# Two query tiles of a pair of heads at once in the attention of a two-layer hybrid block

## The chip, the cores and the metric

The kernel runs on one core of one Trainium2 chip. The metric is the device time of one execution in microseconds; the median of three runs of the kernel before is 2845.89 us (2841.22 to 2847.46).

## What is computed

Two layers over 256 latent tokens x and 256 context tokens ctx, width 1024, all in fp32. The part that matters here is the attention of the mixer, cut from the reference:

```python
for l in range(DEPTH):
    ...                                   # adaLN tables, first feed-forward part
    q, k, v, z, xbc, dt, g = split_in(h @ w_in[l])     # for latents and for context
    # 16 heads of 64; q and k normalised, latents rotated
    # latents: each query sees a window of latent keys (with a bias and a mask) and all context keys
    s_all = concat([q . k_win * scale + bias (or -inf), q . k_ctx * scale])
    o_l = softmax(s_all) . [v_win, v_ctx]
    # context, in layer 0 only: queries see the context keys
    o_c = softmax(q_c . k_c * scale) . v_c
    ...                                   # state-space branch, gates, output, second feed-forward part
```

## The kernel before, in words

Matrix products are made of three products of fp32r halves: `wchunk` (L85 to L92) splits each chunk of weights into a high and a low part, by a copy on ScalarE (L90) and a subtraction on VectorE (L91), and `gemm_t` and `gemm_n` (L114 to L116, L125 to L127) issue three matmuls per step.

PSUM has eight banks. Three form the ring "mm" (`bank`, L130), one the ring "ms" (`bank2`, L133). In attention a score tile "s" has two banks and one buffer, and "o" has two buffers of one bank (`pbank`). A ring hands out a bank for each tile that is asked for and takes it back when the last reader of the tile before is done. The ring "mm" serves qkps (the q, k and v products), qkt (their transposes), gps (gates), dtps (the step sizes of the state-space branch) and nps (the output product with na_w_o). Within block 0 some qkps and qkt tiles take "o" banks instead (L447).

The 16 heads are worked in four blocks of four (L633 to L637). `qkv_block` makes q, k and v of a block from 256 columns of w_in each, normalises and rotates q and k, and transposes them; at its end (L521 to L524) it makes the first q product of the next block ahead. In block 0, `gates(0, 2)` follows; then `attend`. After the four blocks come `dt_prep` and `gates(2, 4)` (L639, L640) and the product with na_w_o (L647).

`attend` takes a pair of heads c, a segment s (0: latent queries against 512 keys; 1: context queries against 256, in layer 0 only) and a query tile qt of 128 at a time. `scores` makes the two score products of the pair (L574; each head has 64 rows of the array), adds the bias and mask for segment 0 (L576), and calls `softmax`: one maximum over both heads (L551), and per head an exponential with its sum (L555), a reciprocal (L556) and a scaling (L557). `outputs` transposes the probabilities in blocks of 128 (L592, into an "ms" bank), copies them to SBUF (L593), and after the second query tile makes the products with v of both heads (L599, into an "o" bank) and splits the result into halves (L330, L331). The loop at L607 calls `scores` one step ahead of `outputs`.

The order of the instructions on each engine is fixed when the program is built. The instructions that are ready go in the order of the program text, so that products traced later stand between pieces of attention that still wait. On TensorE's list the score products of a step wait until the exponentials of the step before have read the score tile.

Of the kernel before, what the change touches and what calls it, by code (L numbers as in the profile page):

```python
# [7 lines left out]
F32 = mybir.dt.float32  # L8
# [3 lines left out]
ALU = mybir.AluOpType  # L12
# [4 lines left out]
P = 128  # L17
# [3 lines left out]
T = 512  # L21
SEG = 256
DFF = 2816
KF = DFF // P
HD = 64
# [31 lines left out]
class Kernel:  # L57
    def __init__(self, tc, I, dbg):
        self.tc, self.nc, self.I, self.dbg = tc, tc.nc, I, dbg
        self.ada_it, self.ada_done, self.wnext = self.ada_all(), (-1, 0), None  # L60

    def dump(self, name, ap):
        if self.dbg is not None and name in self.dbg:
            self.nc.sync.dma_start(self.dbg[name], ap)
# [373 lines left out]
    def qkv_block(self, l, b, ap, tabs, ctx_q, ahead):  # L438


        nc = self.nc
# [4 lines left out]
        qk = ap.tile([P, 4, T], F32, name="qk", tag="qk", bufs=2)  # L446
        v = ap.tile([P, 4, 256], F32, name="v", tag="v", bufs=2)  # L447

        tags = iter("mmmooommmoo" if b == 0 else "m" * 11)

        def bank(n):
            return self.bank(n) if next(tags) == "m" else self.pbank("o", 2)

        def products(t2, w):
            ps = bank("qkps").rearrange("p (a n) -> p a n", a=2)
            for i in range(2):
                self.gemm_n(ps[:, i], w, 0, 256, self.hrhs, slice((2 * t2 + i) * P, (2 * t2 + i + 1) * P))
            return ps

        def finish(t2, a, ps):  # L460

            p3 = ps.rearrange("p t (h d) -> p (t h) d", d=HD)
            sq = ap.tile([P, 2, 256], F32, name="sq", tag="sq").rearrange("p t (h d) -> p (t h) d", d=HD)
            nc.scalar.activation(sq, p3, AF.Square)
            ss = self.sm.tile([P, 8], F32, name="ss", tag="ss")
            nc.vector.tensor_reduce(out=ss, in_=sq, axis=AX.X, op=ALU.add)
            r = self.rstd(ss, 8, HD)
            qn = ap.tile([P, 2, 256], F32, name="qn", tag="qn")
            q3 = qn.rearrange("p t (h d) -> p (t h) d", d=HD)
# [12 lines left out]
            pt = bank("qkt").rearrange("p (c t n) -> p c t n", c=2, t=2)  # L482
            for t in range(2):
                for c in range(2):
                    nc.tensor.transpose(pt[:, c, t], qn[:, t, c * P : (c + 1) * P], self.con("id"))
            o = qk[:, 2 * a : 2 * a + 2, t2 * SEG : (t2 + 1) * SEG].rearrange("p c (t n) -> p c t n", t=2)
            nc.scalar.copy(o, pt[:, :, :, ::-1] if t2 == 0 and a == 0 else pt)
# [55 lines left out]
                                in1=self.con("mask")[:, None, :].to_broadcast([P, 12, GRID]), op=ALU.add)  # L543
        return bt

    def softmax(self, ap, ps, nk):

        nc = self.nc
        mx = self.sm.tile([P, 2], F32, name="mx", tag="mx", bufs=4)
        sm = self.sm.tile([P, 2], F32, name="sme", tag="sme", bufs=4)  # L550
        nc.vector.tensor_reduce(out=mx, in_=ps, axis=AX.X, op=ALU.max, negate=True)  # L551
        out = []
        for a in range(2):
            p = ap.tile([P, T], F32, name="p", tag="p", bufs=3)[:, :nk]
            self.last_exp = nc.scalar.activation(p, ps[:, a], AF.Exp, bias=mx[:, a : a + 1], accum_out=sm[:, a : a + 1]).ins  # L555
            nc.vector.reciprocal(sm[:, a : a + 1], sm[:, a : a + 1])  # L556
            nc.vector.tensor_scalar(out=p, in0=p, scalar1=sm[:, a : a + 1], scalar2=None, op0=ALU.mult)  # L557
            out.append(p)
        return out

    def attend(self, l, b, ap, qk, v, ctx_q, aT):
        nc = self.nc
        units = [(c, s, a, qt) for c in range(2) for s in range(2 if ctx_q else 1) for qt in range(2) for a in range(2)]
        bts, st, pts = {}, {}, {}

        def scores(us):
            c, s, _, qt = us[0]
# [3 lines left out]
            ps = self.pph.tile([P, 2, T], F32, name="ps_s", tag="s", bufs=1)[:, :, : nk * P]  # L571
            for a in range(2):
                o = slice(64 * a, 64 * a + 64)
                nc.tensor.matmul(ps[:, a], qk[o, c, (2 * s + qt) * P : (2 * s + qt + 1) * P], qk[o, 2 + c, s * SEG :], start=True, stop=True)  # L574
            if s == 0:
                nc.vector.tensor_tensor(out=ps[:, :, :SEG], in0=ps[:, :, :SEG],  # L576
                                        in1=bts[c][:, :, 2 - 2 * qt : 6 - 2 * qt].rearrange("p a e k -> p a (e k)"), op=ALU.add)
            for u, p in zip(us, self.softmax(ap, ps, nk * P)):
                st[u] = p

        def outputs(us):

            c, s, _, qt = us[0]
            nk = 4 if s == 0 else 2
            if qt == 0:
                for a in range(2):
                    pts[a] = ap.tile([P, 4, SEG], F32, name="pt", tag="pt", bufs=2)[:, :nk]
            for u in us:
                p = st.pop(u)
                tp = self.bank2("ptp").rearrange("p (j q) -> p j q", j=4)[:, :nk]  # L590
                for j in range(nk):
                    nc.tensor.transpose(tp[:, j], p[:, j * P : (j + 1) * P], self.con("id"))  # L592
                last = nc.scalar.copy(pts[u[2]][:, :, qt * P : (qt + 1) * P], tp[:, :, ::-1] if s == 0 else tp).ins  # L593
            if qt == 1:
                po = self.pbank("o", 2)[:, :SEG]
                for j in range(nk):
                    for a in range(2):
                        hc = (2 * c + a) * HD
                        i = nc.tensor.matmul(po[64 * a : 64 * a + 64], v[:, j + 4 - nk, hc : hc + HD], pts[a][:, j], start=(j == 0),  # L599
                                             stop=(j == nk - 1), tile_position=(0, 64 * a)).ins  # L600
                        if j == a == 0:
                            self.tc.add_manual_dep(i, last.name, mybir.DependencyInfo(
                                mybir.DependencyClass.Sync, mybir.DependencyReason.DATA), reason="pairs")
                self.split(aT[2 * b + c][:, :, s * SEG : (s + 1) * SEG], po)
# [575 lines left out]
```

## Time and profile before

| what | value |
|---|---|
| runs | 2841.22, 2845.89, 2847.46 us; median 2845.89 |
| profiled execution | 2845.74 us, its span 2844.0 us, mean granted clock 0.991 |
| TensorE busy | 2752.6 us, 97% of the span |
| VectorE busy | 2007.0 us, 71% |
| ScalarE busy | 1344.2 us, 47% |
| chain that ended last | TensorE 85%, VectorE 6%, DMA 4%, ScalarE 3% |
| score products (L574) | 96 products, 192 records |
| transposes of p (L592) | 320 records |
| products with v (L599) | 320 records |

An fp32 product appears as two records of the array (two passes), a transpose or an fp32r product as one. A busy TensorE is not TensorE at its peak, as the ends of pipelined matmuls are modelled; distances between starts tell more than durations. "qkps" and the like are the program's names for tiles.

### The profile page before, as it was taken

The page shows a single profiled execution, that of the slowest core. Times are in us where ns is not written, and L with a number is a line of the kernel's source. Part 1 is how long each engine was busy: PE and PEld are TensorE (multiplying, and loading weights), DVE is VectorE, ACT ScalarE, POOL GpSimd, SP SyncE. Part 2 cuts the span into 40 slices and gives each one's busy share as a digit, 9 for nine tenths or more (in the row PEclk, how much of TensorE's full clock was granted, in tenths as well). Part 3 has the DMA queues.
Part 4 walks back from the last instruction along what each step waited for, and adds up shares of the span by engine and source line. Part 5 has one row for each costly group of instructions (what it writes and reads, how often), then busy time and mean ns, then how long its engine had stood idle before and what let it go on. Part 6 is the DMA issues. An engine that isn't in the chain of part 4 may idle for free.

```text
span 2844.0 us, 41229 instructions
## 1 busy us (share of the span) xinstructions
PE 2752.6 (97%) x15748; PEld 2274.6 (80%) x15748; DVE 2007.0 (71%) x3793; ACT 1344.2 (47%) x2453; POOL 76.9 (3%) x132
## 2 busy tenths in 40 slices
PE   7999999999999999998999999999899999999899
PEld 5888888776777777787888898888888787789899
DVE  5995356767479888779963389533687868898654
ACT  4322233544368887643312242222344558777443
POOL 0000010100000000000000000000100000000000
PEclk9999999999999999999999999999999999999999
DMA  8874253321322222365743267432544343335564
GB/s 284 263 242 126 85 157 97 77 55 43 118 73 58 72 63 89 104 207 186 236 155 89 93 197 242 130 94 89 163 114 91 65 144 92 90 117 164 163 186 148
DMA packets 316246, 374.21 MB, mean 132 GB/s; under 512 B 15504, under 2 KB 292368, under 8 KB 315664
## 3 DMA queue, kind: packets, MB, share of 16 engines
q1 hardware_dynamic: 308624, 351.64, 40.5%
q0 software_dynamic: 7424, 19.93, 3.8%
q8 instruction: 124, 2.03, 0.3%
q14 instruction: 74, 0.61, 0.1%
HBM read 363.13 MB, written 8.39 MB: 131 GB/s over the span
## 4 chain that ended last, share of the span: by engine, by line
PE 85%; DVE 6%; DMA 4%; ACT 3%; issue 1%; POOL 0%; SPq 0%; ACTq 0%; DVEq 0%; POOLq 0%
PE pg L115 5%; PE pg L114 5%; PE pg L116 5%; PE pd L116 5%; PE pd L115 5%; PE pd L114 5%; PE pu L115 5%; PE pu L116 5%; PE pu L114 5%; PE xps L114 3%; PE xps L115 3%; PE xps L116 3%; PE ps_y L846 3%; PE qkps L125 2%; PE qkps L127 2%; PE qkps L126 2%
## 5 line engine op out<-in xcount | busy, mean ns | idle before, releaser
L91 DVE TENSOR_TENSOR hl<-raw,hl 128x1024 fp32r<-128x1024 f32 (+1 forms) x538 | 624.1, 1162 | 468.0 <-ACT hl L90 466.5
L90 ACT CAST hl<-raw 128x1024 fp32r<-128x1024 f32 (+1 forms) x538 | 537.1, 1001 | 659.5 <-PE pd L116 246.7
L192 DVE SCALAR_TENSOR_TENSOR junk<-wt,cb 128x1024 f32<-128x1024 f32 x256 | 312.5, 1221 | 7.8 <-DMA wt<-in_w_adt_dram 3.4
L116 PE MATMUL pd<-act,hl 128*128 128x512 f32 (+1 forms) x824 | 277.3, 336 | 0.0
L115 PE MATMUL pd<-act,hl 128*128 128x512 f32 (+1 forms) x824 | 276.6, 336 | 0.0
L114 PE MATMUL pd<-act,hl 128*128 128x512 f32 (+1 forms) x824 | 276.1, 335 | 0.0
L114 PE MATMUL pg<-h,hl 128*128 128x512 f32 (+1 forms) x736 | 264.5, 361 | 8.5 <-ACT h L330 4.8
L116 PE MATMUL pg<-h,hl 128*128 128x512 f32 (+1 forms) x736 | 265.0, 360 | 1.0 <-DVE hl L91 1.0
L115 PE MATMUL pg<-h,hl 128*128 128x512 f32 (+1 forms) x736 | 265.4, 361 | 0.5 <-DVE h L331 0.5
L114 PE MATMUL pu<-h,hl 128*128 128x512 f32 (+1 forms) x696 | 252.9, 364 | 0.7 <-DVE x L325 0.7
L115 PE MATMUL pu<-h,hl 128*128 128x512 f32 (+1 forms) x696 | 253.1, 364 | 0.0
L116 PE MATMUL pu<-h,hl 128*128 128x512 f32 (+1 forms) x696 | 252.8, 363 | 0.0
L126 PE MATMUL qkps<-hl,h 128*128 128x256 f32 x672 | 194.2, 289 | 7.7 <-DVE hl L91 7.7
L125 PE MATMUL qkps<-hl,h 128*128 128x256 f32 x672 | 195.8, 292 | 4.9 <-ACT hl L90 3.8
L127 PE MATMUL qkps<-hl,h 128*128 128x256 f32 x672 | 193.1, 287 | 0.0
L873 DVE SCALAR_TENSOR_TENSOR m<-m,dtn,cbm 128x256 f32<-128x256 f32 (+1 forms) x384 | 144.6, 411 | 36.1 <-ACT m L871 35.6
L115 PEld LDWEIGHTS pd<-act,hl 128*128 128x128 f32 x824 | 154.8, 188 | 18.1
L114 PEld LDWEIGHTS pd<-act,hl 128*128 128x128 f32 x824 | 154.9, 188 | 17.9
L116 PEld LDWEIGHTS pd<-act,hl 128*128 128x128 f32 x824 | 155.0, 188 | 16.5
L114 PEld LDWEIGHTS pg<-h,hl 128*128 128x128 f32 x736 | 138.8, 190 | 33.0 <-ACT h L330 6.5
L115 PEld LDWEIGHTS pg<-h,hl 128*128 128x128 f32 x736 | 139.7, 190 | 24.2 <-DVE h L331 2.2
L116 PEld LDWEIGHTS pg<-h,hl 128*128 128x128 f32 x736 | 139.6, 190 | 24.3 <-DVE hl L91 1.2
(270 smaller groups left out, 5981.9 us busy)
## 6 DMA issues: line engine op xcount, KB each, us to landing
raw<-in_w_in_dram SPq DMA_DIRECT2D x144, 512.0 KB, 3.9
wt<-in_w_adt_dram SPq DMA_DIRECT2D x128, 512.0 KB, 4.4
raw<-in_ffn_w_down_dram SPq DMA_DIRECT2D x92, 512.0 KB, 3.5
raw<-in_ffn_w_gate_dram SPq DMA_DIRECT2D x88, 512.0 KB, 3.9
raw<-in_ffn_w_up_dram SPq DMA_DIRECT2D x88, 512.0 KB, 3.9
raw<-in_ssd_w_o_dram SPq DMA_DIRECT2D x32, 512.0 KB, 3.5
raw<-in_w_out_dram SPq DMA_DIRECT2D x20, 512.0 KB, 4.0
wa<-in_w_ada_dram SPq DMA_DIRECT2D x16, 512.0 KB, 8.9
```

The source lines that it names most:

```text
L90: nc.scalar.copy(hl[:, 0], t)
L91: nc.vector.tensor_tensor(out=hl[:, 1], in0=t, in1=hl[:, 0].bitcast(F32), op=ALU.subtract)
L114: mm(ps, wh, xh[:, cols], start=(first and i == 0), stop=False)
L115: mm(ps, wh, xl[:, cols], start=False, stop=False)
L116: mm(ps, wl, xh[:, cols], start=False, stop=(last and i == len(st) - 1))
L125: mm(ps, xh[:, cols], wh, start=(i == 0), stop=False)
L126: mm(ps, xh[:, cols], wl, start=False, stop=False)
L127: mm(ps, xl[:, cols], wh, start=False, stop=(i == len(st) - 1))
L192: nc.vector.scalar_tensor_tensor(out=self.junk, in0=w, scalar=1.0, in1=self.cb[:, s], op0=ALU.mult, op1=ALU.mult, accum_out=md[:, k, s : s ...
L846: nc.tensor.matmul(*a, **k)
L873: v.scalar_tensor_tensor(out=e[:, o1], in0=e[:, o1], scalar=self.dtn[:, 2 * s + j, r : r + 1], in1=cbm[s][:, d, o1], op0=ALU.mult, op1=ALU ...
```

## The change

`attend` works on a pair of heads and a segment, with both query tiles at once. `scores` issues four score products in a row. For segment 0 they go to two score tiles of two banks each; for segment 1 all four share one tile (each bank holds the two query tiles of a head). The first of the four waits for the last exponential of the unit before, and stands behind the last product with v issued so far. `softmax` takes two heads, or for segment 1 all four rows at once with one maximum. The score tag "s" has two buffers, and "o" is gone: the products with v take a bank of "mm", and so do the transposes of the second head of each query tile. In block 0, qkps and qkt tiles that took "o" banks take halves of "s" tiles. Probability tiles have four buffers for three.

```diff
@@ qkv_block
+        spare = []
+
         def bank(n):
-            return self.bank(n) if next(tags) == "m" else self.pbank("o", 2)
+            if next(tags) == "m":
+                return self.bank(n)
+            if not spare:
+                two = self.pph.tile([P, 2, T], F32, name="ps_o", tag="s", bufs=2)
+                spare.extend([two[:, 1], two[:, 0]])
+            return spare.pop()
@@ softmax
-    def softmax(self, ap, ps, nk):
+    def softmax(self, ap, ps, n):
...
-        for a in range(2):
-            p = ap.tile([P, T], F32, name="p", tag="p", bufs=3)[:, :nk]
+        for a in range(n):
+            p = ap.tile([P, T], F32, name="p", tag="p", bufs=4)[:, :nk]
@@ attend
-        units = [(c, s, a, qt) for c in range(2) for s in range(2 if ctx_q else 1) for qt in range(2) for a in range(2)]
+        units = [(c, s) for c in range(2) for s in range(2 if ctx_q else 1)]
...
+            if s == 0:
+                ps = [self.pph.tile([P, 2, T], F32, name="ps_s", tag="s", bufs=2) for _ in range(2)]
+            else:
+                p4 = self.pph.tile([P, 2, T], F32, name="ps_s", tag="s", bufs=2).rearrange("p a (q n) -> p a q n", q=2)
+                ps = [p4[:, :, qt] for qt in range(2)]
+            for qt in range(2):
+                for a in range(2):
+                    o = slice(64 * a, 64 * a + 64)
+                    i = nc.tensor.matmul(ps[qt][:, a], qk[o, c, ...], qk[o, 2 + c, s * SEG :], start=True, stop=True).ins
+                    if st and qt == a == 0:
+                        self.tc.add_manual_dep(i, self.last_exp.name, ... Sync ...)
+                        if self.last_pv:
+                            self.tc.add_manual_dep(i, self.last_pv.name, ... NoSync ...)
+            for qt in range(2):
+                if s == 0:
+                    nc.vector.tensor_tensor(out=ps[qt][:, :, :SEG], ... bias ...)
+                    for a, p in enumerate(self.softmax(ap, ps[qt], 2)):
+                        st[c, s, qt, a] = p
+            if s == 1:
+                for i, p in enumerate(self.softmax(ap, p4.rearrange("p a q n -> p (a q) n"), 4)):
+                    st[c, s, i % 2, i // 2] = p
...
-                tp = self.bank2("ptp").rearrange("p (j q) -> p j q", j=4)[:, :nk]
+                    tp = (self.bank("ptp") if a else self.bank2("ptp")).rearrange("p (j q) -> p j q", j=4)[:, :nk]
...
-                po = self.pbank("o", 2)[:, :SEG]
+            po = self.bank("ps_o")[:, :SEG]
...
+                    self.last_pv = i
...
-        for i in range(0, len(units) + 2, 2):
+        for i in range(len(units) + 1):
             if i < len(units):
-                scores(units[i : i + 2])
+                scores(units[i])
             if i > 0:
-                outputs(units[i - 2 : i])
+                outputs(units[i - 1])
```

## Rows read from the trace of the kernel before

**Rows 1.** The page: busy time by engine; the chain that ended last by engine.

```profile
PE 2752.6 (97%) x15748; PEld 2274.6 (80%) x15748; DVE 2007.0 (71%) x3793; ACT 1344.2 (47%) x2453; POOL 76.9 (3%) x132
...
PE 85%; DVE 6%; DMA 4%; ACT 3%; issue 1%; POOL 0%; SPq 0%; ACTq 0%; DVEq 0%; POOLq 0%
```

**Rows 2.** Windows of both attention stretches: length, busy time by engine with records.

```profile
core 0: us, PE busy (x) PEld busy (x) DVE busy (x) ACT busy (x) POOL busy (x), PEclk, DMA share, GB/s
492.00:727.10 235.10, 224.86 (x1519) 170.59 (x1518) 167.15 (x411) 119.85 (x278) 15.53 (x24) 1.00 0.29 61
2102.60:2273.70 171.10, 164.30 (x1217) 134.41 (x1216) 132.25 (x290) 87.31 (x169) 15.81 (x24) 1.00 0.40 83
sum 406.20, PE 389.16 PEld 305.00 DVE 299.40 ACT 207.16 POOL 31.34; mean PE 194.58 PEld 152.50 DVE 149.70 ACT 103.58 POOL 15.67
```

**Rows 3.** Timeline of TensorE in block 0 of layer 0: start, duration, line.

```profile
523.18 1.13 PE L574 MATMUL ps_s<-qk 64*128 64x512 f32 x4
524.24 0.66 PE L592 MATMUL ptp<-c_cst,p 128*128 128x128 f32 x4
524.65 0.36 PE L127 MATMUL qkps<-hl,h 128*128 128x256 f32 x1
...
525.63 0.66 PE L592 MATMUL ptp<-c_cst,p 128*128 128x128 f32 x4
...
528.36 0.70 PE L574 MATMUL ps_s<-qk 64*128 64x256 f32 x4
...
531.73 0.70 PE L574 MATMUL ps_s<-qk 64*128 64x256 f32 x2
532.36 1.95 PE L599 MATMUL ps_o<-pt,v 128*64 128x256 f32 x16
534.23 0.70 PE L574 MATMUL ps_s<-qk 64*128 64x256 f32 x2
534.86 0.44 PE L592 MATMUL ptp<-c_cst,p 128*128 128x128 f32 x2
```

**Rows 4.** Windows of TensorE where products stand alone (256, then 512 columns).

```profile
659.90:669.20 9.30, 9.30 (x80) 1.00 0.33 89
727.00:768.00 41.00, 41.00 (x180) 1.00 0.39 122
```

**Rows 5.** Timeline of TensorE at the start of block 3's attention, layer 0.

```profile
669.17 0.60 PE L485 MATMUL qkt<-c_cst,qn 128*128 128x128 f32 x4
671.37 0.63 PE L485 MATMUL qkt<-c_cst,qn 128*128 128x128 f32 x4 [1.60 <-DVE qn L481]
671.75 0.47 PE L114 MATMUL dtps<-h,hl 128*64 128x512 f32 x1
```

**Rows 6.** Timeline of VectorE: the second chunk of dtps's weights is split.

```profile
625.63 0.42 DVE L91 TENSOR_TENSOR hl<-raw,hl 128x256 fp32r<-128x256 f32 x1
```

**Rows 7.** Timeline of ScalarE: the copy of v out of its bank.

```profile
669.37 0.59 ACT L490 COPY v<-qkps 128x512 f32<-128x512 f32 x1 [4.17 <-PE qkps L127]
```

**Rows 8.** Groups by line and form, 492 to 727: count, busy us, mean ns, idle before.

```profile
L551 DVE TENSOR_REDUCE mx<-ps_s 128x2 f32<-128x1024 f32 x16 | 19.5, 1220 | 0.3
...
L593 ACT COPY pt<-ptp 128x512 f32<-128x512 f32 x32 | 18.8, 588 | 25.6 <-PE ptp L592 25.6
...
L557 DVE TENSOR_SCALAR p<-p,sme 128x512 f32<-128x512 f32 x32 | 15.3, 482 | 0.9
...
L555 ACT ACTIVATE p<-ps_s,mx 128x256 f32<-128x256 f32 x32 | 15.0, 475 | 2.7 <-DVE mx L551 1.9 <-PE ptp L592 0.7
...
L576 DVE TENSOR_TENSOR ps_s<-ps_s,bt 128x512 f32<-128x512 f32 x16 | 11.1, 694 | 7.0 <-PE ps_s L574 7.0
```

**Rows 9.** Line L555, the exponentials: ns least, median, most.

```profile
L555 ACT ACTIVATE p<-ps_s,mx x96: 465/682/704, 499.2 to 2261.2; 128x512 f32<-128x512 f32 x64, 128x256 f32<-128x256 f32 x32
L555 ACT ACTIVATION_READ_ACCUMULATOR p<-ps_s,mx x96: 190/200/220, 499.7 to 2261.8; 128x1 f32 x96
...
L555 ACT ACT_TABLE_LOAD  x2: 1283/1283/1283, 497.9 to 2110.5; - x2
```

**Rows 10.** Windows with idle stretches of TensorE; PEclk is the granted clock.

```profile
1298.00:1303.00 5.00, 0.40 (x4) 0.20 (x2) 5.00 (x16) 0.00 (x0) 0.00 (x0) 1.00 0.70 215
1303.00:1310.00 7.00, 4.98 (x21) 4.71 (x22) 6.96 (x19) 2.62 (x6) 0.00 (x0) 0.52 0.48 153
2106.00:2113.00 7.00, 4.62 (x40) 4.42 (x38) 4.43 (x6) 3.84 (x6) 0.00 (x0) 1.00 0.77 217
```

More of the change, by code (lines that the diff above doesn't have):

```diff
@@ L562, in attend, with scores @@
         nc = self.nc
[L563 to L567 removed]
+        units = [(c, s) for c in range(2) for s in range(2 if ctx_q else 1)]
+        bts, st = {}, {}
+        def scores(u):
+            c, s = u
             nk = 4 if s == 0 else 2
@@ L578, in scores @@
[L578 to L583, printed above, removed]
+                ps = [self.pph.tile([P, 2, T], F32, name="ps_s", tag="s", bufs=2) for _ in range(2)]
[5 more added lines that the diff above has]
+                    o = slice(64 * a, 64 * a + 64)
+                    i = nc.tensor.matmul(ps[qt][:, a], qk[o, c, (2 * s + qt) * P : (2 * s + qt + 1) * P], qk[o, 2 + c, s * SEG :], start=True, stop=True).ins
+                    if st and qt == a == 0:
+                        self.tc.add_manual_dep(i, self.last_exp.name, mybir.DependencyInfo(
+                            mybir.DependencyClass.Sync, mybir.DependencyReason.DATA), reason="pairs")
+                        if self.last_pv:
+                            self.tc.add_manual_dep(i, self.last_pv.name, mybir.DependencyInfo(
+                                mybir.DependencyClass.NoSync, mybir.DependencyReason.DATA), reason="pairs")
@@ new lines, in scores @@
+            for qt in range(2):
+                if s == 0:
+                    nc.vector.tensor_tensor(out=ps[qt][:, :, :SEG], in0=ps[qt][:, :, :SEG],
+                                            in1=bts[c][:, :, 2 - 2 * qt : 6 - 2 * qt].rearrange("p a e k -> p a (e k)"), op=ALU.add)
+                    for a, p in enumerate(self.softmax(ap, ps[qt], 2)):
[3 more added lines that the diff above has]
+                    st[c, s, i % 2, i // 2] = p
@@ L584, in outputs @@
+        def outputs(u):
+            c, s = u
             nk = 4 if s == 0 else 2
-            if qt == 0:
+            pts = [ap.tile([P, 4, SEG], F32, name="pt", tag="pt", bufs=2)[:, :nk] for _ in range(2)]
+            for qt in range(2):
                 for a in range(2):
-                    pts[a] = ap.tile([P, 4, SEG], F32, name="pt", tag="pt", bufs=2)[:, :nk]
-            for u in us:
-                p = st.pop(u)
-                tp = self.bank2("ptp").rearrange("p (j q) -> p j q", j=4)[:, :nk]
-                for j in range(nk):
-                    nc.tensor.transpose(tp[:, j], p[:, j * P : (j + 1) * P], self.con("id"))
-                last = nc.scalar.copy(pts[u[2]][:, :, qt * P : (qt + 1) * P], tp[:, :, ::-1] if s == 0 else tp).ins
@@ L594, in outputs @@
-            if qt == 1:
-                po = self.pbank("o", 2)[:, :SEG]
[L596 to L604, printed above, removed]
@@ L607, in attend @@
-        for i in range(0, len(units) + 2, 2):
+                    p = st.pop((c, s, qt, a))
+                    tp = (self.bank("ptp") if a else self.bank2("ptp")).rearrange("p (j q) -> p j q", j=4)[:, :nk]
+                    for j in range(nk):
+                        nc.tensor.transpose(tp[:, j], p[:, j * P : (j + 1) * P], self.con("id"))
+                    last = nc.scalar.copy(pts[a][:, :, qt * P : (qt + 1) * P], tp[:, :, ::-1] if s == 0 else tp).ins
+            po = self.bank("ps_o")[:, :SEG]
@@ new lines, in outputs @@
+            for j in range(nk):
+                for a in range(2):
+                    hc = (2 * c + a) * HD
+                    i = nc.tensor.matmul(po[64 * a : 64 * a + 64], v[:, j + 4 - nk, hc : hc + HD], pts[a][:, j], start=(j == 0),
+                                         stop=(j == nk - 1), tile_position=(0, 64 * a)).ins
+                    if j == a == 0:
+                        self.tc.add_manual_dep(i, last.name, mybir.DependencyInfo(
+                            mybir.DependencyClass.Sync, mybir.DependencyReason.DATA), reason="pairs")
+                    self.last_pv = i
@@ L608, in attend @@
+            self.split(aT[2 * b + c][:, :, s * SEG : (s + 1) * SEG], po)
+        for i in range(len(units) + 1):
             if i < len(units):
-                scores(units[i : i + 2])
+                scores(units[i])
             if i > 0:
-                outputs(units[i - 2 : i])
+                outputs(units[i - 1])
     def attention(self, l, ctx_q, nao, dp):
```

12 lines of the change are left out of this document (4 added, 8 removed).

## The prediction

> **What bounds the kernel now.** I read the page first, then the two attention stretches by windows, then TensorE's timeline in them. TensorE is busy 97% of the span and the chain of waits lies on it for 85% [rows 1], so what TensorE does, or waits for, in these stretches is what the change can move. The stretches run from the first score product to the last wait of attention in layer 0 (492.0 to 727.1, 235.1 us) and in layer 1 (2102.6 to 2273.7, 171.1 us), 406.2 us together. TensorE is busy for 389.2 us of them and VectorE for 299.4 (74%) [rows 2]: TensorE is the bound there too, because products of the next block and of the gates ("the fill") stand between the pieces of attention. One call of two score products takes 1.06 us (523.18 to 524.24), four transposes 0.41 (524.24 to 524.65), sixteen records with v 1.87 (532.36 to 534.23) [rows 3]. Fill alone runs at 9.3 / 80 = 0.116 us a record for 256 columns and 41.0 / 180 = 0.228 for 512 [rows 4]. Between pieces of attention six records take 0.98 (524.65 to 525.63) where six at 0.116 are 0.70 [rows 3]: each return to the fill costs 0.28 us. And of nine calls the two halves stand apart, with the products with v between them: 0.63 at 531.73 and again at 534.23 [rows 3].
>
> **The change, part by part.**
>
> *Fewer turns.* A unit (pair of heads, segment) had two score calls, four batches of transposes and one of products with v; now one call, batches that can stand in pairs (two rings for them), one batch with v. If the fill stays where it is, about two returns per unit go: 24 units x 2 x 0.28 = 13.4 us. Inside a call, 1.06 us are two passes of 512 columns, which at the pace of the products with v (1.87 us for 8 passes of 256) are 0.94; joined calls save 0.12 each, 24 x 0.12 = 2.9. The nine torn calls (seven of 256 columns, two of 512) give back 7 x 0.63 + 2 x 1.06 = 6.5. Together 23 us, were nothing else to change.
>
> *The common ring.* This is the part that I think decides. Products with v had banks of their own ("o") and the transposes one ("ms"); now the products with v and every second transpose tile take banks of the ring "mm", which is also the ring of every fill product (qkps, qkt, gps, dtps, nps). The trace shows how that ring hands out banks: in the order in which the program asks. At 669.77 TensorE falls idle for 1.60 us, until the four transposes into qkt at 671.37, and the products into dtps start right behind them at 671.75 [rows 5]. dtps waited for none of its data: its weights had been split by 626.05 (625.63 + 0.42) [rows 6], and the bank of v came free with the copy that ended at 669.96 [rows 7]. It stood idle behind qkt because qkt was asked for earlier. Attention of block b is called (L637) ahead of the q, k and v products of block b+1 (L634 of the next turn) and of dt_prep and gates (L639, L640). So in the changed kernel the first fill product behind attention of block b can start only when the last product tile with v of that block has started. What was asked for before (the next block's first q product, and in block 0 two gate chunks) comes before attention starts, as now. Attention then runs without fill, at the length of its own chain.
>
> *That chain.* With little beside it, a two-product call repeats after 5.18 us (523.18 to 528.36) [rows 3]; its steps are product 1.06, bias 0.69, maximum 1.22, two exponentials 1.38 and the accumulator's read 0.20 [rows 8, 9], 4.55 in all, so 0.63 are handovers and foreign work. A four-product unit of segment 0 waits (the new wait on the last exponential) for 1.06 + 2 x 1.91 + 1.38 + 0.20 + 0.63 = 7.1 us; for twice the handovers I take 7.4. A unit of segment 1 has 1.06, one maximum of 1.22, four exponentials of 0.475, read and handovers: 5.0, and 5.2 with the products with v that must stand ahead of the next call. Layer 0, four units: 7.4 + 5.2 + 7.4 + 5.0, then scaling 0.5, transposes 0.4, copy 0.4, handovers 0.6 and eight records with v 1.0: 28 us a block. Layer 1, two units: 7.4 + 7.1, then scaling 0.65, transposes 0.8, copy 0.6, handovers 0.6 and sixteen records 1.87: 19 us. TensorE's own work in it, at the pace of [rows 3], is some 17 and 11 us; the rest is idle, and it is new. The 23 us above are hidden in it: turns cost nothing beside a wait.
>
> *The fill behind it.* Of the 1519 records of layer 0's stretch 4 x 128 are attention's, 1007 are not; 132 of these have 512 columns (dtps 24, gates 96 by the code, the first dozen with na_w_o): 132 x 0.228 + 875 x 0.116 = 131.6 us. Layer 1: 1217 - 4 x 80 = 897, 24 of them wide: 106.7 us [rows 2, 4]. At each of six block starts the first call waits for the copy of qk with nothing beside it, and products that used to be spread follow each other and wait for their banks: 2 us each, an estimate (qkt alone cost 1.60 at 669.77 [rows 5]), 6 us a layer. The table load of 1.28 us [rows 9] ahead of the first exponential loses its cover in each layer.
>
> Layer 0: 4 x 28 + 131.6 + 6 + 1.3 = 250.9 against 235.1, +15.8. Layer 1: 4 x 19 + 106.7 + 6 + 1.3 = 190.0 against 171.1, +18.9. Sum +34.7.
>
> *The clock.* After 5 us with 0.40 us of work (1298 to 1303) the granted clock stood at 0.52, the level of 1.2 GHz, from 1303 to 1310; with 4.62 us of work in 7 (2106 to 2113) it stayed at 1.00 [rows 10]. Behind each block's first call TensorE would stand idle for some 4 us. One fall per block that costs 1 us of its chain is 8 us; none is 0, and falls in most units would be 30. I take 8.
> The Trainium skill (TensorE: Matmul & The Clock Gate, Part 1) says that the slow clock is the idle state and that activity releases it; by that rule every wait of the new chain invites a fall, which is the rival below, and the trace bears it out in one of the two stretches named.
>
> *Small parts.* Four p tiles for three: exponentials wait for p tiles that the transposes of the unit before release, and these stand ahead; nothing. In block 0 of each layer the score tiles lend their halves to qkt and k; all are copied before the first call: nothing, at most one handover of 0.2. DMA issues, bias loads and their order stay.
>
> The profiled execution is 2845.74 us (span 2844.0); 2845.7 + 34.7 + 8 = 2888.4. The median of the runs shown lies 0.15 above: 2889.
>
> **Bounds.** Without foreign work the units take 6.5 and 4.5, a block 24.5 and 16.8, a start 0.5: +2.9, 2849. With as much foreign work as VectorE's 74% allow, 8.5 and 6, blocks of 31.8 and 21.2, starts of 3 us: +65, and with 30 for the clock 2940.
>
> **Rivals.**
> - *The fill stays* (faster). If a fill product may take a bank while attention tiles asked for before it wait, 23 us go and some 8 return, as products and attention share three banks: 2845.9 - 15 = 2831. For it: 9 torn calls and some 48 returns are real [rows 3]. Against it: 1.60 us of idleness with a ready product [rows 5 to 7]. It decides if fill records stand inside the changed attention stretches.
> The Trainium skill (Perfetto Trace Analysis, Optimizing Tensor Performance, Matmuls) says that independent groups should rotate through different banks, so that emptying one overlaps the next; by that rule alone the wider choice of banks is this rival, 2831. No row of before shows it for this ring.
> - *The chain is as short as its steps.* Attention alone, with VectorE and ScalarE freed of the fill's work, costs what its turns cost now: 2849 to 2862. For it: foreign work is a tenth of the 5.18. Against it: the splitting of prefetched weights (1.2 us each on VectorE) falls into it.
> - *The clock falls in most units*: 2845.9 + 35 + 30 and more waits, 2915 to 2940. For it: idle stretches of some 4 us in each block. Against it: 1.00 at 2106 to 2113.
>
> **Chances.** Forecast (2862 to 2915) 0.58, short chain 0.17, clock 0.13, fill stays 0.12. A measurement of this kernel tells about 0.2% (5.7 us) from no change. Faster by more: 0.12; within: 0.08 (the low end of the short chain); slower: 0.80. Range 2849 to 2935; the forecast's own is 2862 to 2915.
>
> **What would show it.** Right: in the attention stretches no qkps, gps or dtps records between score calls, TensorE's idle time there up from 17 us to 60 or more and ended by exponentials and scaling, score calls some 7 us apart, all products of the next block packed behind the last products with v, no torn calls. Wrong: fill records between the calls; or calls 5 us apart; or clock well below 1.00 there, which would make the size wrong and the step right.

## The result and the profile after

The changed kernel takes 2941.11 us (median of 5 runs, 2938.29 to 2942.00), the kernel before 2847.46 beside it (5 runs, 2841.22 to 2850.24): a ratio of 1.0327 with an interval of [1.0315, 1.0339]. That is 94 us more, where 43 were forecast, and 6 us beyond the upper end of the range. The profiled execution has a span of 2939.3 us (2844.0 before).

Of the 95.3 us between the spans, 56.8 arise from layer 0's attention up to the first score call of layer 1 (491.6 to 2159.0, before 492.0 to 2102.6 [rows 2]) and 38.9 from there to the end (ahead of that attention the changed kernel is 0.4 shorter).

The page of the changed kernel, busy time of TensorE and the chain that ended last by engine, to set beside [rows 1]:

```profile
PE 2767.6 (94%) x15748; PEld 2290.2 (78%) x15748; DVE 2012.3 (68%) x3785; ACT 1350.8 (46%) x2459; POOL 77.0 (3%) x132
...
PE 85%; DVE 6%; ACT 4%; DMA 3%; issue 1%; POOL 0%; SPq 0%; DVEq 0%; ACTq 0%; POOLq 0%
```

TensorE has the same number of records and is busy for 15.0 us more. A busy share that falls from 97% to 94% says that it waits more; busy time that rises with the same work says that some of it ran slower.

Windows of the changed kernel (columns as in [rows 2]): attention of layer 0 from the first score call to the last products with v, one block of it, the products behind that block, and attention of layer 1.

```profile
491.60:748.10 256.50, 202.98 (x1378) 159.57 (x1378) 146.46 (x354) 107.50 (x261) 15.71 (x24) 0.88 0.25 48
567.30:604.90 37.60, 24.47 (x128) 14.47 (x128) 24.51 (x62) 17.07 (x51) 5.15 (x8) 0.82 0.26 22
604.90:642.60 37.70, 36.53 (x306) 35.78 (x304) 19.68 (x47) 11.84 (x17) 0.00 (x0) 1.00 0.24 64
2159.00:2345.20 186.20, 146.86 (x1030) 118.23 (x1029) 108.17 (x237) 74.36 (x150) 15.76 (x24) 0.89 0.32 62
```

The reader is to see three things. A block's attention now stands alone, with its 128 records and nothing else, and 304 records of the next blocks' products stand packed behind it (the other two of the 306 are the end of the last products with v). TensorE idles for 53.5 + 39.3 = 93 us in the two stretches, against 17 before [rows 2]. And the granted clock is 0.82 inside the block and 1.00 behind it; before it was 1.00 in both stretches [rows 2].

TensorE's timeline in block 1 of layer 0, changed kernel (start, duration, line, idle time before and what ended it):

```profile
567.34 1.99 PE L590 MATMUL ps_s<-qk 64*128 64x512 f32 x8 [0.73 <-ACT qk L495]
574.84 1.11 PE L618 MATMUL ptp<-c_cst,p 128*128 128x128 f32 x4 [5.52 <-DVE p L566]
575.99 2.08 PE L590 MATMUL ps_s<-qk 64*128 64x256 f32 x8
578.00 2.82 PE L618 MATMUL ptp<-c_cst,p 128*128 128x128 f32 x12
581.95 0.41 PE L618 MATMUL ptp<-c_cst,p 128*128 128x128 f32 x2 [1.13 <-DVE sme L565]
582.95 1.95 PE L624 MATMUL ps_o<-pt,v 128*64 128x256 f32 x16 [0.58 <-ACT pt L619]
584.83 1.99 PE L590 MATMUL ps_s<-qk 64*128 64x512 f32 x8
...
591.87 2.08 PE L590 MATMUL ps_s<-qk 64*128 64x256 f32 x8
593.87 1.93 PE L618 MATMUL ptp<-c_cst,p 128*128 128x128 f32 x12
598.49 0.66 PE L618 MATMUL ptp<-c_cst,p 128*128 128x128 f32 x2 [2.68 <-ACT pt L619]
599.07 3.16 PE L624 MATMUL ps_o<-pt,v 128*64 128x256 f32 x16
...
603.92 1.08 PE L624 MATMUL ps_o<-pt,v 128*64 128x256 f32 x8 [0.74 <-ACT pt L619]
604.94 0.38 PE L126 MATMUL qkps<-hl,h 128*128 128x256 f32 x1
```

The four products of a call stand together, no call is torn, and no fill stands between the calls; all of that against [rows 3]. The steps from call to call are 8.65, 8.84 and 7.04 us, and 13.1 from the last call to the end of the block, where 7.4, 5.2, 7.4 and 7.9 were forecast. The same records appear in two lengths: sixteen records with v take 1.95 us at 582.95 and 3.16 at 599.07.

### The profile page after: what moved, and what is told of

The parts are those of the page before. It is cut to its first block, busy times and chain, and to the rows that moved or that the text cites. A ratio compares the mean times of both kernels' runs of the same rounds, so it can differ in the third digit from the quotient of the medians.

```text
span 2939.3 us, 41178 instructions
## 1 busy us (share of the span) xinstructions
PE 2767.6 (94%) x15748; PEld 2290.2 (78%) x15748; DVE 2012.3 (68%) x3785; ACT 1350.8 (46%) x2459; POOL 77.0 (3%) x132
## 4 chain that ended last, share of the span: by engine, by line
PE 85%; DVE 6%; ACT 4%; DMA 3%; issue 1%; POOL 0%; SPq 0%; DVEq 0%; ACTq 0%; POOLq 0%
PE pg L115 5%; PE pg L116 5%; PE pg L117 5%; PE pu L117 5%; PE pu L116 5%; PE pd L117 5%; PE pd L116 5%; PE pu L115 5%; PE pd L115 5%; PE xps L115 3%; PE xps L116 3%; PE xps L117 3%; PE qkps L126 3%; PE qkps L128 3%; PE qkps L127 2%; PE ps_y L871 2%
## 5 line engine op out<-in xcount | busy, mean ns | idle before, releaser
L126 PE MATMUL qkps<-hl,h 128*128 128x256 f32 x672 | 192.6, 287 | 6.4 <-ACT hl L91 3.8
L127 PE MATMUL qkps<-hl,h 128*128 128x256 f32 x672 | 191.1, 284 | 7.2 <-DVE hl L92 7.2
L128 PE MATMUL qkps<-hl,h 128*128 128x256 f32 x672 | 190.7, 284 | 0.0
```

Source lines behind the costliest of these rows:

```text
L126: mm(ps, xh[:, cols], wh, start=(i == 0), stop=False)
L127: mm(ps, xh[:, cols], wl, start=False, stop=False)
L128: mm(ps, xl[:, cols], wh, start=False, stop=(i == len(st) - 1))
```

## Experiments: what stops the fill

**Only the products with v moved.** In the kernel before:

```diff
-                po = self.pbank("o", 2)[:, :SEG]
+                po = self.bank("ps_o")[:, :SEG]
```

> The kernel before with one edit: the products with v take a bank of the common ring; calls of two score products, one score tile and transposes in their own bank stay. Theory A (the common ring serves in the order of asking, so fill can't stand inside attention): no fill records between the score calls, TensorE idle there as in the changed kernel; a block has twice as many calls as in the changed kernel at about 5 us each, so 2900 to 2960. Rival B (the four-product unit itself costs the time, and the ring is innocent): within 10 us of the kernel before, 2836 to 2856, with fill between the calls.

Measured: 3048.7 us, 1.0715 [1.0691, 1.0739]. Windows of both attention stretches of this kernel:

```profile
493.40:800.10 306.70, 232.12 (x1378) 161.01 (x1378) 152.79 (x362) 111.43 (x261) 15.48 (x24) 0.81 0.20 39
2209.00:2445.50 236.50, 176.76 (x1030) 127.15 (x1030) 112.20 (x238) 75.84 (x150) 15.47 (x24) 0.75 0.25 49
```

Another ring for this one tile costs 203 us, more than the whole change, and beyond theory A's range. The stretches hold the 1378 and 1030 records of the changed kernel, with no fill between the calls; the granted clock is 0.81 and 0.75, and attention has twice as many calls to wait for. Theory A holds for the mechanism; B falls. (Differences between runs of different sets are taken by their ratios to the kernel before, which ran beside each; a thousandth is 2.8 us.)

**All attention tiles but the scores taken out of the common ring.** In the changed kernel:

```diff
-                    tp = (self.bank("ptp") if a else self.bank2("ptp"))...
+                    tp = self.bank2("ptp")...
-            po = self.bank("ps_o")[:, :SEG]
+            po = self.bank2("ps_o")[:, :SEG]
```

> The changed kernel with one part undone: all transposes of the probabilities and the products with v take the one small bank, none the common ring; four score products in a row and two score tiles stay. Theory A: fill stands inside attention again, granted clock 1.00 there, and the time falls back to 2825 to 2850. Rival B: fill or not, the four-product unit keeps the time above 2900.

Measured: 2846.8 us against 2845.1, 0.9998 [0.9988, 1.0008]. Windows of both attention stretches of this kernel:

```profile
493.40:716.20 222.80, 210.11 (x1490) 164.99 (x1489) 165.53 (x401) 118.85 (x276) 15.69 (x24) 1.00 0.31 64
2099.60:2266.10 166.50, 154.76 (x1146) 127.91 (x1145) 118.10 (x252) 83.91 (x164) 15.98 (x24) 0.98 0.38 76
```

The records are back (1490 instead of 1378 in layer 0), and so is the clock. The whole loss of 94 us hangs on the ring; joined calls and two score tiles, with the transposes and the products with v crowded into one bank, cost nothing and bring nothing.

**Only the second transposes in the common ring.** As above, but the first of the two edits left out.

> The changed kernel with the products with v in the small bank, and every second transpose tile in the common ring as it is. Theory A (each tile of attention in that ring stops the fill until it has its turn): fill enters only behind the last of these tiles, 9 to 17 records ahead of a block's last products with v, and the time stays near the changed kernel's, 2915 to 2945. Rival K (only the products with v hold the fill up): 2840 to 2860.

Measured: 2938.9 us, 1.0324 [1.0308, 1.0339]. The transposes alone do the whole damage here, as the products with v alone did in the kernel before. K falls. Every tile of attention in that ring holds up the fill that is asked for behind it; taking one kind out while the other stays gives nothing back.

**The asking order changed, the banks left.** Attention of a block and the next block's products (in the last block gates and dt) are asked for in turns:

```diff
-                self.attend(l, b, ap, qk, v, ctx_q, aT)
+                for _ in self.attend(l, b, ap, qk, v, ctx_q, aT):   # yields ahead of outputs()
+                    next(nxt, None)                                 # one product of block b + 1
```

> The changed kernel with the asking order changed and nothing else: attention of a block and the products of the next block (in the last block dt and the gates) are asked for in turns, one piece each. Theory A: the ring is no obstacle when fill is asked for between the units; one lump of 48 records (5.6 us) stands beside each unit's chain, the clock stays at 1.00, and few turns are left: 2795 to 2830, faster than both. Rival E (three banks are too few for lumps and attention together, so that units wait behind lumps or lumps behind units): 2840 to 2880.

Measured: 2946.0 us, 1.0354 [1.0339, 1.0369]; both theories missed it. What TensorE waited for in layer 0 of this kernel (us in total, times, longest):

```profile
PE ptp L623 <- ACT pt L624: 20.8, 15, 2.3
PE dtt L762 <- DVE dtmp L730: 15.3, 1, 15.3
PE ps_o L629 <- ACT pt L624: 7.9, 9, 1.3
```

The fill came back, but whole lumps of it are asked for ahead of the transposes, and the transposes then wait for each other's copies. And dt, asked for ahead of the last outputs, blocks TensorE for 15.3 us behind its own chain on VectorE. So another order of asking alone took nothing back. It was tried again with more: fill behind each unit, attention's instructions first where both can run, dt at the end, and the mask addition behind the products with v (below).

> The changed kernel with the tiles in the common ring as they are; one product of the next block (gates in the last) is asked for behind each unit instead of all behind the block, attention's instructions go first where both could run, and the mask addition comes behind the products with v. Theory A (it was the asking order, not the number of banks): fill stands in all waits, granted clock 1.00, 2800 to 2845. Rival E (three banks shared by lumps, transposes and outputs are too few): waits at transposes and outputs remain, 2860 to 2930.

Measured: 2864.2 us, 1.0058 [1.0041, 1.0074], 77 us less than the changed kernel with the same tiles in the same ring. The granted clock is 1.00 in layer 0. So most of the loss can be taken back with every tile left in the ring. How much of that the asking order gives by itself is not shown: the run before, with that alone, gave nothing, and here attention's instructions go first as well, among them the copies, which are worth 23 us alone in the changed kernel (below; the mask edit alone is worth nothing there). Yet 17 us stay, 5.2 of them waits of the products with v for copies in layer 0, and the time lies in rival E's range, at its low end: A has the kind of loss, E the size of what is left.

> As the run before it, with all transposes in the one small bank and only the products with v in the common ring. Theory A: 2800 to 2845. Rival E: if the banks were too few for transposes and fill, this one is clearly faster than the run before it; if both stand above 2860, the products with v alone hold the fill up.

Measured: 2883.8 us, 1.0129 [1.0113, 1.0145]: 20 us slower than the run before it. A choice of banks for the transposes helps once fill is let in; crowding by transposes, which rival E supposed, is not what remains. Both runs stand above 2860, which by the expectation leaves the products with v; a run of this version with them alone out of the ring is missing.

## Experiments: why attention alone is longer than forecast

Attention alone takes 38.0, 37.7, 37.4 and 34.8 us in layer 0 and 28.5, 22.2, 26.4 and 21.4 in layer 1 (first score product to last product with v), 148 and 98.5 us, where 112 and 76 were forecast.

**The clock.** Twenty unread records behind the first call of a block and eight ahead of each group of products with v, in a bank of the ring:

```diff
+        def idle(n):
+            d = self.bank("idle")
+            for i in range(n):
+                nc.tensor.matmul(d, self.h[0][:, 0, :P], self.h[0][:, 0, :], start=(i == 0), stop=(i == n - 1))
```

> The changed kernel with products that nobody reads put into TensorE's waits inside attention (20 records of 512 columns behind the first score call of a block, 8 ahead of the products with v of each unit); the order of everything else stays. Theory C (half of the missed size is the clock: records in attention run at 1.2 GHz, 9.6 us a block in layer 0 and some 4 us in layer 1, 54 us in all, most of it on the chain): granted clock above 0.95 in the attention stretches, blocks of 28 to 32 and 19 to 22 us, 2885 to 2910. Rival D (the chain is longer through VectorE's and ScalarE's steps, and the clock only slows records that have time): the clock rises, and the time stays at 2925 or more.

Measured: 2937.5 us, 1.0325 [1.0308, 1.0343]. Windows of layer 0 and of its block 1:

```profile
491.60:744.20 252.60, 232.59 (x1586) 185.13 (x1586) 145.66 (x354) 106.60 (x261) 15.69 (x24) 0.98 0.25 48
566.40:604.30 37.90, 31.83 (x178) 20.18 (x177) 23.98 (x62) 16.90 (x51) 5.16 (x8) 0.95 0.26 22
```

The clock rose from 0.88 to 0.98, and this block took 37.9 us, as without (37.7). The 54 us of theory C are not there, and the time is where D has it. But D holds only in the main: over all eight blocks attention takes 237.8 us in this trace and 246.4 in the changed kernel's, 8.6 less, which the times don't show, as their intervals reach some 5 us either way.

**The mask addition.** VectorE adds the mask to a later unit's bias table as soon as its queue comes to it, and it waits there for the table's load. In the changed kernel, block 1 (VectorE):

```profile
580.38 0.96 DVE L550 TENSOR_TENSOR bt<-bt,c_att 128x768 f32<-128x768 f32 x1 [1.04 <-DMA bt<-in_na_rpb_dram]
581.26 0.16 DVE L565 RECIPROCAL sme<-sme 128x1 f32<-128x1 f32 x1
581.45 0.35 DVE L566 TENSOR_SCALAR p<-p,sme 128x256 f32<-128x256 f32 x1
```

Put behind the products with v of the unit before (`add_manual_dep` on `last_pv`):

> The changed kernel with one more dependence: the addition of the mask to the next bias table on VectorE comes behind the products with v of the unit before (in the changed kernel it stands in VectorE's queue ahead of the scaling of a segment-1 unit and waits there for its load). Theory F (that wait and the 0.96 us of the addition lie on the chain, twice a block in layer 0): 10 to 20 us less, 2920 to 2931. Rival G (the copies of the transposes behind the exponentials on ScalarE end last anyway): within 5 us of the changed kernel, 2936 to 2945.

Measured: 2939.7 us, 1.0326 [1.0310, 1.0342]. Nothing in the time, as G has it; the eight blocks take 239.8 us in the trace, 6.6 less, none of it in this block (37.6).

**Copies behind exponentials.** ScalarE in the same block of the changed kernel:

```profile
579.15 0.58 ACT L619 COPY pt<-ptp 128x512 f32<-128x512 f32 x1 [2.57 <-PE ptp L618]
580.00 0.58 ACT L619 COPY pt<-ptp 128x512 f32<-128x512 f32 x1 [0.27 <-PE ptp L618]
580.48 0.48 ACT L564 ACTIVATE p<-ps_s,mx 128x256 f32<-128x256 f32 x1
...
582.29 0.60 ACT L619 COPY pt<-ptp 128x512 f32<-128x512 f32 x1
```

The fourth copy of unit 0 stands behind the four exponentials of unit 1. The products with v at 582.95 wait for it, and the next call at 584.83 stands behind them in TensorE's queue. The copies were given priority:

```diff
+                    with self.tc.high_priority(offset=300):
                         last = nc.scalar.copy(pts[a]...
```

> The changed kernel with one edit: the copies of the transposes go first on ScalarE where both they and an exponential could run. Theory G (in the changed kernel the fourth copy of a unit stands behind the four exponentials of the next, and its products with v wait for it): TensorE's waits for those copies, 25.5 us in both layers, mostly go; 2905 to 2925. Rival J (limits of nearly equal length lie beside each other, so that taking one away brings up the next, as it was with the clock and the mask addition): 2930 or more.

Measured: 2916.8 us, 1.0245 [1.0228, 1.0262], 23 us less than the changed kernel. ScalarE and VectorE of this kernel in the same block:

```profile
577.42 0.59 ACT L620 COPY pt<-ptp 128x512 f32<-128x512 f32 x1 [2.57 <-PE ptp L618]
578.27 1.07 ACT L620 COPY pt<-ptp 128x512 f32<-128x512 f32 x2 [0.27 <-PE ptp L618]
579.23 0.49 ACT L564 ACTIVATE p<-ps_s,mx 128x256 f32<-128x256 f32 x1
```

```profile
592.80 0.96 DVE L550 TENSOR_TENSOR bt<-bt,c_att 128x768 f32<-128x768 f32 x1 [2.00 <-DMA bt<-in_na_rpb_dram]
593.68 0.22 DVE L565 RECIPROCAL sme<-sme 128x1 f32<-128x1 f32 x2
```

All copies now stand ahead of the exponentials, and the time is in G's range; J's 2930 or more falls. The waits that G named did not mostly go, though: TensorE's waits of the products with v for copies fall from 25.5 to 16.0 us. The rest of the gain is not idle time alone, as the windows of both attention stretches show:

```profile
491.30:730.20 238.90, 194.43 (x1378) 155.16 (x1378) 145.83 (x354) 107.77 (x260) 15.51 (x24) 0.91 0.26 51
2138.60:2318.10 179.50, 143.95 (x1030) 116.25 (x1030) 107.86 (x237) 73.89 (x150) 15.62 (x24) 0.91 0.33 64
```

TensorE's idle time is 80 us instead of 93, and its busy time for the same records 11.5 us shorter, at a granted clock of 0.91 instead of 0.88 and 0.89. So a part of the 23 us may be the clock's; the two were not separated. In block 1 the mask addition has come up: it waits 2.00 us for its load, and the scaling of the last unit stands behind it. That is what J expects, and the three were taken away together:

> The changed kernel with three edits together: unread products in TensorE's waits, the mask addition behind the products with v, copies first on ScalarE. Rival J: alone none of them gave much, together they bring the blocks near the forecast lengths, 28 to 31 us in layer 0 and 19 to 22 in layer 1: 2885 to 2910. If it stays above 2920, the missed length is in none of the three but in the steps of VectorE and the handovers between engines.

Measured: 2925.0 us, 1.0270 [1.0251, 1.0288], above both bounds, and slower than the copies alone. By the expectation that would clear all three edits; the two runs below speak against it: without the unread records the same edits are 11 us faster, and with three instead of eight ahead of every group of products with v another 8. The eight were no longer in a wait but in the way. So the sum was built up again, one edit at a time:

> The changed kernel with copies first on ScalarE and the mask addition behind the products with v. With the copies in front, VectorE's waits for the load of the bias (1.0 and 2.0 us in block 1 of layer 0) stand ahead of the scaling that the last outputs wait for. Theory J (limits side by side): now the mask addition counts, 8 to 14 us less than with the copies alone: 2903 to 2909. Rival: it counts nothing again, 2913 to 2920.

Measured: 2911.0 us, 1.0230 [1.0216, 1.0244], 4 less than with the copies alone, at half of J's lower bound and between the two ranges; the intervals overlap, so the time alone does not show it. The trace has it where J puts it: in the first three blocks of layer 0 the step from the last call to the end falls from 10.3, 9.5 and 8.9 us to 7.7 each.

> As the run before it, with unread products in TensorE's waits, 20 records behind the first call of a block and only 3 (0.7 us) ahead of each group of products with v, so that they take little of the chain themselves. Theory C in what is left of it (records at 1.2 GHz on the chain): 8 to 15 us less than the run before it, 2890 to 2900. Rival D (the clock slows records that have time): within 4 us of it, or slower.

Measured: 2903.4 us, 1.0203 [1.0189, 1.0217], 7.7 less than the run before it on the same chip, just short of theory C (8 to 15) and outside D (4 at most). The granted clock rises with it from 0.93 and 0.92 in the two stretches to 1.00 and 0.97. TensorE's timeline in block 1 of this kernel:

```profile
561.61 1.99 PE L598 MATMUL ps_s<-qk 64*128 64x512 f32 x8
...
570.14 1.13 PE L598 MATMUL ps_s<-qk 64*128 64x256 f32 x8 [0.49 <-ACT p L567]
571.20 1.53 PE L626 MATMUL ptp<-c_cst,p 128*128 128x128 f32 x12
572.49 0.94 PE L583 MATMUL idle<-h 128*128 128x512 f32 x3
573.51 1.95 PE L634 MATMUL ps_o<-pt,v 128*64 128x256 f32 x16
575.39 1.99 PE L598 MATMUL ps_s<-qk 64*128 64x512 f32 x8
...
582.79 1.14 PE L598 MATMUL ps_s<-qk 64*128 64x256 f32 x8
...
589.61 1.08 PE L634 MATMUL ps_o<-pt,v 128*64 128x256 f32 x8
590.62 0.39 PE L126 MATMUL qkps<-hl,h 128*128 128x256 f32 x1
```

The steps are 8.5, 5.3, 7.4 and 7.8 us. The last three have the lengths of the forecast's 5.2, 7.4 and 7.9 in a kernel in which three things are out of the way that were not. Term by term they are not its chain: in the second step TensorE goes without a break through the call, twelve transposes, the three unread products and the sixteen records with v, and the last exponential ends only 0.2 us ahead of the next call, so that 5.3 is as much TensorE's own work as the chain. The first step is 8.5 to 8.7 us in block 1 of all these versions, where 7.4 were forecast, as VectorE normalises and rotates the next block's first q product (L478, L484) among the bias additions and maxima. In the changed kernel:

```profile
569.45 0.69 DVE L478 TENSOR_TENSOR qn<-qkps,rs_y 128x512 f32<-128x512 f32 x1
570.06 0.69 DVE L600 TENSOR_TENSOR ps_s<-ps_s,bt 128x512 f32<-128x512 f32 x1
570.65 0.41 DVE L484 TENSOR_TENSOR sq<-qn,sg 128x256 f32<-128x256 f32 x1
570.99 1.22 DVE L560 TENSOR_REDUCE mx<-ps_s 128x2 f32<-128x1024 f32 x1
```

No run took that work away.

The eight blocks together take 246.4 us in the changed kernel's trace. Alone, the three edits take off 8.6 (unread products), 6.6 (mask addition late) and 26.3 (copies first), 41.5 in all; in a row they come to 214.9 and then 205.6, 40.8 less than the changed kernel. So in the traces, one execution each, the three add up. That one hides behind another, as J supposes, is seen in block 1, where the first two do nothing alone, and is not shown for the sum: the times (nothing, nothing and 23 alone, 35 in a row) differ from it by about what their intervals allow.

## Experiments: a version that beats both

All in the version with transposes and products with v in the one small bank. With the mask addition late:

> Transposes of the probabilities and products with v in the one small bank (as in the run in which the common ring was undone), and the mask addition behind the products with v as well. Theory F: the waits of the transposes, 22 us in both layers there, fall by a third to a half: 2832 to 2840. Rival H (these waits are set by the one bank and ScalarE's order, the load is hidden beside fill): 2843 to 2850.

Measured: 2842.2 us, 0.9978 [0.9970, 0.9987]. Two tenths of a per cent, between the two ranges: theory F's sign at half its size. With the copies first as well:

> The version with all transposes and products with v in the one small bank and the mask addition behind the products with v, and the copies of the transposes first on ScalarE as well. Theory G: some of its 20 us of waits at transposes go, 2830 to 2839. Rival: with fill beside them the waits are hidden already, and it stays at 2839 to 2846.

Measured: 2840.5 us, 0.9977 [0.9968, 0.9985]: the rival. Beside fill, the copies' order was covered. With both heads of a segment-1 unit in one transpose tile:

> The version with all attention tiles but the scores in the one small bank, mask addition behind the products with v and copies first, and the transposes of both heads of a segment-1 unit in one bank and one copy: 16 returns to the fill less in layer 0 (4.5 us at 0.28) and 16 copies less. If returns count: 2832 to 2838. If the waits of the one bank set the pace: 2838 to 2843.

Measured: 2840.6 us, 0.9984 [0.9975, 0.9993]: fewer copies bring nothing. In the trace TensorE turns from attention to fill 64 times in layer 0 (77 in the version before), 13 returns fewer and not 16. The time fits the second reading, that the waits of the one bank set the pace and a return costs nothing where TensorE would wait anyway; it was not tested further. In these versions layer 0 is shorter and layer 1 longer than before. In layer 1, with segment 0 alone, the one bank still waits (one wait of 4.7 us for VectorE, 3.9 for copies). So layer 0 was taken as in the second of these and layer 1 as before:

> Layer 0 as in the version with all transposes and products with v in the one small bank, mask addition behind the products with v and copies first; layer 1 as in the kernel before (calls of two products, products with v in banks of their own). In the earlier runs layer 0 was 8.7 to 9.5 us shorter than before and layer 1 4.6 to 5.6 longer. If the two layers are independent: 2834 to 2839. If what layer 0 gains is given back behind it: 2840 to 2846.

Measured: 2835.6 us against 2846.9, 0.9966 [0.9953, 0.9978], faster than the kernel before by 11 us and than the changed one by 103 (0.9966 against 1.0327). Layer 0 takes 267.1 us from its first score call to the last product of its output projection, where the kernel before takes 276.6.

## Why the prediction was wrong, step by step

*Common ring: right, and shown.* One tile of attention in that ring is enough, transposes or products with v; the same tiles cost 77 us less once fill is asked for behind each unit and attention's instructions go first. The rival "the fill stays" falls: a block of 128 records holds attention's alone. The Trainium skill's advice that the prediction weighed (Perfetto Trace Analysis, Optimizing Tensor Performance, Matmuls), to rotate independent groups through different banks, is no rule against a shared ring, but here the runs decide what it leaves open: two users of one ring are independent only if the order of asking lets them be.

*Fewer turns: 23 us were too many.* With the fill back (the run with all tiles but the scores out of the ring), joined calls are worth nothing over both layers. No call is torn there, but the returns, 13.4 of the 23 us, did not become fewer: TensorE turns from attention to fill 75 times in layer 0 and 40 in layer 1 before, and 76 and 43 times there, where one bank leaves the batches of transposes no pairs. With two rings for them and fill behind each unit it is 58 and 22 times, and the kernel is still slower than before (1.0058). In layer 0 the span from the first call to the end of the output projection falls by 6.3 us (276.6 to 270.3), in layer 1 it grows by 6.8 (187.1 to 193.9). TensorE waits at transposes in both layers, some 21 us together against 4 before; that four exponentials come where there were two, and one bank serves for all, are the likely reasons and were not separated.

*That chain: the step that failed.* "Attention alone", put at 28 and 19 us a block, measured 37.0 and 24.6 in the mean, 58 us over the forecast in all. The other terms together miss by some 5 us (95.3 - 34.7 - 58.4, and 2.6 for the two table loads, which fall into the blocks). The forecast took score call to exponentials to next score call as the chain, and let the transposes, copies and products of the unit before run beside it, with 0.2 us for the products with v ahead of a next call. They stand in the same instruction lists of TensorE and ScalarE as the chain. Copies behind exponentials on ScalarE were worth 23 us (a part perhaps by the clock), the mask addition on VectorE some 4 behind that (within the intervals), the clock 8 behind both, 35 together. That a call stands behind the products with v is part of the change itself and was not undone in any run. What is left, a ratio of 1.0203 or 58 us, stands against 34.7 in the forecast without its clock term: 23 us. By the trace of that run 4 of it lie in the blocks of layer 0 (117.4 against 112 and the table load of 1.3), 11 in those of layer 1 (88.2 against 76 and 1.3), and the remaining 8 or so outside attention. In the first block of layer 1, ScalarE's weight casts wait for their load and VectorE's splits stand ahead of the bias addition; this was read from the trace and not tested.

*"Small parts: nothing."* The mask addition stood in front of the scaling, where its wait for the load counts. Putting it late was worth some 6 us with fill beside it (0.9998 to 0.9978), nothing in the time without fill, and some 4 without fill behind the copies. So it was worth something with fill beside it as well, where the forecast had it at nothing.

*The clock.* Forecast 8 us, bounds 0 to 30; measured 7.7 at the end of the row of edits, and nothing in the time at its beginning (1.0325 against 1.0327; 8.6 in the blocks of the trace). That the sizes agree is luck: 8 was one fall a block that costs 1 us of its chain, and the condition was the rival's, and one of the signs of being wrong. At 0.88 and 0.89, the clock stood at 1.2 GHz for (1 - 0.88) x 2 x 256.5 + (1 - 0.89) x 2 x 186.2 = 103 us of the two stretches, idle time included. It happened in most units and cost little, so most slow records must have had time; which of them had is not shown. The sign said that the clock would make the size wrong; the runs give it 8 or 9 of the 58 us by which the blocks are too long, and whatever part of the copies' 23 is its own. The rule of the Trainium skill (TensorE: Matmul & The Clock Gate, Part 1), that the slow clock is the idle state and activity releases it, agrees with these rows: 0.82 in a block with 13 us of idle time, 1.00 in the packed products behind it, 0.98 with unread products in the waits.

*Sum.* The bounds' upper end, 2940, came from more foreign work on VectorE and 30 us of clock. The kernel came out near that by luck and in the main for another reason, the order of two kinds of work on ScalarE, which no term held.

## What to carry to other kernels

A ring of buffers that a long chain and its filler share gives the filler nothing until the chain has had its turn: give the chain a bank of its own, or ask for the filler between the chain's steps and let the chain go first. When work loses its cover, write down every in-order queue that it passes and who stands in front on it, on ScalarE and VectorE too, not only the data dependences. And read an edit's effect in the trace of its stretch as well as in the time: here two edits looked like nothing in times that are known to some 5 us, and took 9 and 7 us off the blocks of their traces.

## What the hardware showed that was not expected

The clock stood at 1.2 GHz for 103 us of the attention stretches, and with unread products that brought it back to 0.98 the blocks became 8.6 us shorter and the time changed by less than can be measured. And unread products don't come free: eight of 512 columns are 1.8 us at the pace of [rows 4], and once the waits around them had shrunk, the run with them was 11 us slower than the same edits without (1.0270 against 1.0230), while three in each place made it 8 us faster.
